# The delta rule's stores and reloads issued from ACT instead of SP, in a hybrid encoder layer

## The chip, the cores and the metric

The kernel runs on one core of a Trainium2 chip. The core has five engines that run their own instruction streams in order: PE (TensorE, matrix products), DVE (VectorE), ACT (ScalarE), POOL (GpSimd) and SP (SyncE, which here issues transfers and computes nothing). Transfers between the chip's large memory (DRAM below) and the engines' memory are carried out by 16 DMA engines; an instruction on SP or ACT only issues them. Engines wait for each other, and for transfers, through semaphores.

The metric is device time in microseconds, from one launch. Before the change three runs gave 1266.28, 1262.38 and 1264.82 us, a median of 1264.82.

## What is computed

One layer over 2048 positions of width 1024, in float32. A normalised input is projected, and the projection is split between two groups of heads that read the same rows. Group A is a gated delta rule with four heads, run forward and backward over the sequence; group B is windowed attention. Both are gated, joined, projected back and added to the input. The change lies in group A, whose core is this:

```python
k_beta = k * beta[..., None]
m = jnp.where(strict, jnp.einsum('bhncd,bhnsd->bhncs', k_beta, k) * decay, 0.0)
t_inv = lax.linalg.triangular_solve(eye + m, eye_like_m, left_side=True, lower=True, unit_diagonal=True)
...
def step(state, inp):
    q_i, k_i, u_i, w_i, g_i, a_i = inp
    v_new = u_i - jnp.einsum('bhcd,bhde->bhce', w_i, state)
    o = (jnp.einsum('bhcd,bhde->bhce', q_i * jnp.exp(g_i)[..., None], state)
         + jnp.einsum('bhcs,bhse->bhce', a_i, v_new))
    ...
_, o = lax.scan(step, state0, xs)
```

For each chunk of the sequence a unit triangular matrix `eye + m` has to be inverted before the scan over chunks can use it. The kernel works with chunks of 128 positions, so 16 chunks, in two directions, for each of four heads.

## The kernel before

**Phase A** (to about 690 us of the profile) projects, convolves and does the attention. It is not touched by the diff, except that its instructions are ordered by the same planner. **Phase B** does the delta rule and the output projection. For each head `h` it has these parts, and the parts of one head are interleaved with the scan of the head before:

- `pre_front(h)`: in four groups of four chunks, transposes k and q, forms Gram products on PE (`gh`), and on DVE the matrices `ma` (L711), which hold for each chunk and direction the decayed `m` and the decayed q-k product. Tiles of `ma` stand also under the names `xhi_h` and `xlo_h` for heads 1 and 3, where they lie in space that phase A has left. L716 stores the `m` part of each group and direction to the DRAM tensor `m_d`: 8 stores a head, 32 in all.
- `solve(h)`: inverts the 32 x 32 diagonal blocks of all chunks at once. Two loads read the blocks back from `m_d`, laid out with one row of blocks to a partition: `X` (L739, forward) and `L` (L740, backward), each in pieces of 32 numbers. Then 31 steps on DVE (L749, L753) solve column by column, and L754 stores the result `X` to the DRAM tensor `x_d`.
- `invert(h)`: for each of four groups, loads the solved blocks of both directions into `xc` (L765, 8 loads a head, 32 in all), spreads them over block-diagonal tiles `iv` (DVE and POOL), and builds the full inverse with products on PE (`pi`, L781) and copies on ACT (`b` L790, `iv` L796 and L802, `ma` L799 and L805).
- `scan(h)`: for 16 chunks in each direction `kqc` is loaded (L819), and then PE, DVE and ACT take turns: `pk`, `r`, `py`, `yk` and `y` (ACT, L835 and L837), `po`, the new state `S`.
- `post(h)`: normalises and gates the scan's output `oacc` and stores it (`zt`, `mix_dn`).

As filler between them stand the late gate projections (`zs`, `zhi`, `pf_z`, up to about 790 us) and units of the attention's output projection: `mxs` (load, L583), `mhs` (ACT) and `mls` (DVE), `pcs` (PE), the residual rows `xrs` (load, L593; added on DVE, L599), `part` (store, L600).

**What sets the order.** The program is recorded in the order of the source. Then `set_order` gives each instruction a modelled cost, and simulates a list of ready instructions per engine, forward and backward in turns. The order that it ends with is fixed for every engine. Before the change all 927 DMAs are on SP. The planner takes 500 for the cost of an instruction of SP, adds a lag until the data are there, and lets one shared bus hold SP back when more than it can move is pending. The built program gives each DMA one of eight semaphores (`DMAHW0` to `DMAHW7`) in rotation, so that a DMA's list of waits may name the semaphore of an earlier transfer beside its own data.

Of the kernel before, what the change touches and what calls it, by code (L numbers as in the profile page):

```python
# [15 lines left out]
P = 128  # L16
# [530 lines left out]
def phase_b(ctx, wide, xe, ae, late, tc, t, ident, consts, hp, mix_dn, mix_sw, kq_d, v_d, zdn_d, zsw_d, dp, out):  # L547
    nc = tc.nc
    V, A, G, T = nc.vector, nc.scalar, nc.gpsimd, nc.tensor
    dma = nc.sync.dma_start  # L550

    def pool(name, bufs=1, stack=ctx, **kw):
        return stack.enter_context(tc.tile_pool(name=name, bufs=bufs, reuse_waits="tile", **kw))
# [87 lines left out]
    def pre_front(h):  # L641
# [9 lines left out]
        ma = H["ma"] = {}  # L651
        m_d = dp.tile([2, NCH, 4 * (32 * P + 32)], F32, tag="m_d", name=f"m_d{h}", bufs=2)
        x_d = dp.tile([2, NCH, P, 32], F32, tag="x_d", name=f"x_d{h}", bufs=2)
        for n, c4 in enumerate(FRONT):
            s4 = slice(4 * c4, 4 * c4 + 4)
            cs = slice(c4 * 512, (c4 + 1) * 512)
            kq = q2[:, 2 * (n % 2) : 2 * (n % 2) + 2]
            dma(kq, kq_d[h][:, :, cs])
            vt = q2[:, 4 + n % 2]
            dma(vt, v_d[h][:, cs])  # L660
            gms = []
            for d in range(2):
                k = 2 * (n % 2) + d
                if k < 3:
                    gm = q3[:, k].rearrange("p (c i) -> p c i", c=4)
                else:
                    gm = q1.tile([P, 4, P], F32, tag="gm", name=f"dc{h}_{c4}_{d}", bufs=1)
                if h < NDEC:
                    dma(gm.rearrange("p c i -> p (c i)"), dec_d[h, d][c4])
                else:  # L670
                    src = gr_d[d].rearrange("(c h) i -> c h i", h=4)[s4, h]
                    dma(gm, src.partition_broadcast(P))
                    G.tensor_tensor(gm, gm, dmask[:, d : d + 1].to_broadcast([P, 4, P]), ALU.add)
                gms.append(gm)
                p = 3 - c4 if d else c4
                if p not in mp:
                    mp[p] = ma_tile(h, p)
                ma[d, c4] = mp[p][:, :, 1 - d :: 2]
            for j, ss in ((0, ssk), (1, ssq)):
                tr = ps_t.tile([P, 4, P], F32, tag="tr", name=f"tr{h}_{c4}_{j}")  # L680
                for c in range(4):
                    T.transpose(tr[:, c], kq[:, j, c * P : (c + 1) * P], ident)
                if j == 0:
                    ks[c4] = kv_tile("ks", h, n, f"ks{h}_{c4}")
                    A.activation(ks[c4], tr, AF.Copy)
                for c in range(4):
                    cc = 4 * c4 + c
                    src = ks[c4] if j == 0 else tr
                    jk = q1.tile([P, P], F32, tag="jk", name=f"jk{h}_{c4}_{j}_{c}", bufs=3)
                    A.activation(jk, src[:, c], AF.Square, accum_out=ss[:, cc : cc + 1])  # L690
            V.tensor_scalar(ssk[:, s4], ssk[:, s4], EPS, None, ALU.add)  # L691
            G.tensor_tensor(nk[:, s4], ssk[:, s4], pw[:, 0, :4], ALU.pow)  # L692
            V.reciprocal(ssk[:, s4], ssk[:, s4])
            V.tensor_tensor(
                bp[:, :, s4], beta[:, s4, h :: 4].rearrange("p c d -> p d c"),
                ssk[:, s4].unsqueeze(1).to_broadcast([P, 2, 4]), ALU.mult,
            )
            for c2 in range(2):
                gh = ps_g.tile([P, 2, 2, P], F32, tag="gh", name=f"gh{h}_{c4}_{c2}")
                for k in range(2):  # L700
                    c = 2 * c2 + k
                    T.matmul(
                        gh[:, k], kq[:, 0, c * P : (c + 1) * P], kq[:, :, c * P : (c + 1) * P], start=True, stop=True
                    )
                for k in range(2):
                    c = 2 * c2 + k
                    cc = 4 * c4 + c
                    for d in range(2):
                        if h >= NDEC:
                            A.activation(gms[d][:, c], gms[d][:, c], AF.Exp, bias=ngc[:, d, cc, h : h + 1])  # L710
                        V.scalar_tensor_tensor(  # L711
                            ma[d, c4][:, c], gh[:, k], bp[:, d, cc : cc + 1],
                            gms[d][:, c : c + 1].to_broadcast([P, 2, P]), ALU.mult, ALU.mult,
                        )
            for d in range(2):
                dma(m_d[d, s4, : P * P].rearrange("u (i j) -> i u j", j=P), ma[d, c4][:, :, 0])  # L716
            tr = ps_t.tile([P, 4, P], F32, tag="tr", name=f"trv{h}_{c4}")
            for c in range(4):
                T.transpose(tr[:, c], vt[:, c * P : (c + 1) * P], ident)
            vs[c4] = kv_tile("vs", h, n, f"vs{h}_{c4}")  # L720
            for c in range(4):
                cc = 4 * c4 + c
                A.activation(vs[c4][:, c], tr[:, c], AF.Copy, scale=nk[:, cc : cc + 1])
            if h:
                for k in range(FILLF[h - 1][n]):
                    fill(1, bank(k % 2))
# [6 lines left out]
    def solve(h, H):  # L733
        m_d, x_d, _ = H["solve"]
        L = qa.tile([P, 32, 32], F32, tag="L", name=f"L{h}")
        X = qa.tile([P, 32, 32], F32, tag="X", name=f"X{h}")
        lv = [m_d[d].rearrange("u (p y) -> (u p) y", p=4)[:, : 32 * P] for d in range(2)]
        lv = [a.rearrange("q (r x) -> q r x", x=P)[:, :, :32] for a in lv]
        dma(X[0:64], lv[0])  # L739
        dma(L[64:128], lv[1])  # L740
        x = X.rearrange("p r c -> p (r c)")
        V.tensor_copy(L[0:64], X[0:64].rearrange("p r c -> p c r"))
        G.memset(x, 0.0)
        G.memset(x[:, ::33], 1.0)
        for c in range(31):
            n = 31 - c
            tm = qa.tile([P, 256], F32, tag="tm", name=f"tm{h}_{c}")
            tv = tm[:, : n * (c + 1)].rearrange("p (r k) -> p r k", k=c + 1)
            V.tensor_tensor(  # L749
                tv, L[:, c + 1 :, c : c + 1].to_broadcast([P, n, c + 1]),  # L750
                X[:, c : c + 1, 0 : c + 1].to_broadcast([P, n, c + 1]), ALU.mult,
            )
            V.tensor_tensor(X[:, c + 1 :, 0 : c + 1], X[:, c + 1 :, 0 : c + 1], tv, ALU.subtract)  # L753
        dma(x_d.rearrange("d u (p r) c -> (d u p) (r c)", p=4), X.rearrange("p r c -> p (r c)"))  # L754

    def invert(h, H):
        _, x_d, mp = H["solve"]
        for hi in range(4):
# [3 lines left out]
            for d, c4 in ((0, hi), (1, 3 - hi)):  # L762
                xc = qb.tile([P, 4, 32], F32, tag="xc", name=f"xc{h}_{d}_{c4}", bufs=4)
                xt = qb.tile([P, 4, 32], F32, tag="xt", name=f"xt{h}_{d}_{c4}", bufs=4)
                dma(xc, x_d[d, 4 * c4 : 4 * c4 + 4].rearrange("u i c -> i u c"))  # L765
                V.transpose(xt.rearrange("p u c -> p (u c)"), xc.rearrange("p u c -> p (u c)"))
                x0[d], x1[d] = (xc, xt) if d == 0 else (xt, xc)
            g = qb.tile([P, 4, P], F32, tag="g", name=f"g{h}_{hi}", bufs=2)
# [276 lines left out]
def set_order(tc):  # L1045
# [12 lines left out]
    def aps(l):  # L1058
        return [a.bass_ap for a in l if hasattr(a, "bass_ap")]
# [138 lines left out]
    def cost(i, eng):  # L1198
        o = aps(i.outs)
        m, ins = size(o[0]), aps(i.ins)  # L1200
        if eng == "SP":
            return 500
        if eng == "PE":
            if i.is_transpose:
# [21 lines left out]
    eng = [e for _, e in insts] + [None] * (total - n)  # L1226
    move, late = [0.0] * total, [0.0] * total
    nxt, prv = [[] for _ in range(total)], [[] for _ in range(total)]
    for k in range(total):
        if eng[k] == "SP":  # L1230
            a = aps(insts[k][0].outs)[0]
            count = a.ap[0][1] * size(a)
            piece = min(run(x) for x in aps(insts[k][0].ins) + [a])
            move[k] = count / piece * (8 + 0.148 * piece) / 16
            spread = [x.ap[0][0] == 0 for x in aps(insts[k][0].ins)]
            late[k] = 2000 * any(spread)
        lag = LAG[eng[k]] + move[k] + late[k] if k < n else 0
        if eng[k] == "PE" and not insts[k][0].is_transpose and "float32r" not in str(insts[k][0].ins[0].dtype):
            lag += 40
        if eng[k] == "Activation" and len(aps(insts[k][0].outs)) > 1:  # L1240
            lag += 90
        for s in succ[k]:
            if eng[s] == eng[k] != "SP":
                nxt[k].append((s, SAME[eng[k]] * ((k, s) in wrote)))
            else:
                nxt[k].append((s, lag))
        for s in started[k] if k < n else ():
            nxt[k].append((s, None))
        for s, d in nxt[k]:
            prv[s].append((k, d))  # L1250
# [30 lines left out]
    def plan(order, forward):  # L1281
# [29 lines left out]
        for _ in range(n):  # L1311
# [13 lines left out]
            if e == "SP":  # L1325
                release(k, max(t, bus))
                bus = max(t, bus) + move[k]
                free[e] = max(free[e], bus - 1000)
            else:
                release(k, t)  # L1330
        end = max(free.values())
# [85 lines left out]
```

## Time and profile before

| | before |
|---|---|
| median of three runs | 1264.82 us (1262.38 to 1266.28) |
| profiled execution, span of the core | 1268.0 us, no other time is shown for it |
| mean granted clock of PE | 0.989 |
| DMAs issued on SP, on ACT | 927, 0 |
| moved by them | 206 MB, 163 GB/s over the span |

The span runs from the first to the last instruction. In the views quoted below, "idle before, releaser" means how long an engine had nothing to do ahead of an instruction, and what ended this. `SPq` is SP's sequencer, whose rows are the issues of DMAs; their length is the time that the issue took, not the time to the data's arrival, which the profile gives as "DMA to landing". Matrix products of the profile overlap, so that a busy PE need not be PE at its best; a granted clock under 1 slows it further. The chain is the work that ended last, followed back from the last instruction: a transfer that stands in it was, at that time, what everything else waited for.

### The profile page before, as it was taken

Reading aid. Unit: us, or ns where it says so; the run is one execution under the profiler, and the core shown is the slowest. Engines: PE = TensorE matmul, PEld = TensorE weight load, DVE = VectorE, ACT = ScalarE, POOL = GpSimd, SP = SyncE. Lnnn points to the kernel's source line nnn. Section 1 sums busy time; section 2 is a strip of 40 time slices with the busy share of each in tenths; the row PEclk is TensorE's granted clock in tenths of the full one; section 3 lists DMA queues with packets and bytes.
Section 4 is the critical chain, followed back from the end, with each engine's and each line's share of the span. In section 5 each row is a group of like instructions: output and inputs, shape, how many; then the busy total and the mean of one; then the engine's idle time right before and its main releaser. Section 6 shows DMA issues by size and latency. Waiting matters only on the chain.

```text
span 1268.0 us, 22351 instructions
## 1 busy us (share of the span) xinstructions
PE 1210.5 (95%) x7018; PEld 1037.4 (82%) x7018; DVE 953.7 (75%) x2320; ACT 725.8 (57%) x2167; POOL 529.2 (42%) x845
## 2 busy tenths in 40 slices
PE   6999999999999999999999998999889899999898
PEld 5998888788889988887777777888789689888776
DVE  4523689999854379999995587698769779876765
ACT  6432476666534367766665438658557845685421
POOL 2243454763302276556422304613742441670541
PEclk9999999999999999999999999999889999999999
DMA  7553243513544434431016848967955875854785
GB/s 259 172 160 125 75 154 100 173 60 102 166 145 125 144 110 137 137 96 55 34 51 207 238 141 245 264 189 207 268 166 174 236 200 152 242 175 122 238 269 199
DMA packets 232294, 206.39 MB, mean 163 GB/s; under 512 B 49137, under 2 KB 181873, under 8 KB 232177
## 3 DMA queue, kind: packets, MB, share of 16 engines
q1 hardware_dynamic: 232176, 204.97, 53.0%
q8 instruction: 56, 0.92, 0.3%
q14 instruction: 62, 0.50, 0.1%
HBM read 139.84 MB, written 65.08 MB: 162 GB/s over the span
## 4 chain that ended last, share of the span: by engine, by line
PE 67%; DVE 13%; DMA 9%; ACT 4%; issue 3%; POOL 1%; SPq 1%; DVEq 0%; ACTq 0%; POOLq 0%
PE pf_c L199 5%; PE pf_c L201 5%; PE pf_c L200 5%; PE pf_z L199 4%; PE pf_z L200 4%; PE pf_z L201 4%; PE pi L781 3%; PE pq_q L212 2%; PE pq_q L211 2%; PE pt L390 2%; PE pq_q L210 2%; DMA xc<-x_d 2%; PE py L830 2%; PE po L839 2%; PE pcs L596 2%
## 5 line engine op out<-in xcount | busy, mean ns | idle before, releaser
L199 PE MATMUL pf_c<-xhi,wh_c 128*128 128x512 f32 x384 | 155.7, 405 | 0.8 <-DVE acc L269 0.8
L200 PE MATMUL pf_c<-xlo,wh_c 128*128 128x512 f32 x384 | 154.7, 403 | 0.0
L201 PE MATMUL pf_c<-xhi,wl_c 128*128 128x512 f32 x384 | 154.3, 402 | 0.0
L269 DVE SCALAR_TENSOR_TENSOR acc<-pf_c,cw,acc 128x512 f32<-128x512 f32 (+1 forms) x192 | 140.8, 742 | 2.6 <-POOL acc L259 0.7
L385 POOL TENSOR_SCALAR pr<-pr,st 128x384 f32<-128x384 f32 (+1 forms) x128 | 79.4, 639 | 98.0 <-DVE st L383 71.2
L394 ACT ACTIVATE ph<-pt 128x512 fp32r<-128x512 f32 x92 | 53.0, 595 | 60.5 <-PE pt L390 51.5
L376 ACT ACTIVATE pr<-pr,st 128x384 f32<-128x384 f32 (+1 forms) x128 | 76.2, 597 | 17.8 <-DVE st L372 17.4
L199 PEld LDWEIGHTS pf_c<-xhi,wh_c 128*128 128x128 f32 x384 | 72.5, 189 | 13.5 <-DVE acc L269 1.3
L201 PEld LDWEIGHTS pf_c<-xhi,wl_c 128*128 128x128 f32 x384 | 72.3, 188 | 12.9
L200 PEld LDWEIGHTS pf_c<-xlo,wh_c 128*128 128x128 f32 x384 | 72.4, 188 | 11.6
L835 ACT ACTIVATE yk<-py,ck 128x128 f32<-128x128 f32 x120 | 43.9, 366 | 62.0 <-PE py L830 61.2
L372 DVE CUSTOM_DVE_ANT_0 pr<-s,mask,sink 128x384 f32<-128x384 f32 (+1 forms) x128 | 73.4, 593 | 2.5 <-PE s L371 1.0
L211 PE MATMUL pq_q<-wh_q,xlo 128*128 128x256 f32 x256 | 72.1, 282 | 0.0
L212 PE MATMUL pq_q<-wl_q,xhi 128*128 128x256 f32 x256 | 71.9, 281 | 0.0
L210 PE MATMUL pq_q<-wh_q,xhi 128*128 128x256 f32 x256 | 71.4, 280 | 0.0
L390 PE MATMUL pt<-ident,pr 128*128 128x128 f32 x368 | 69.5, 274 | 1.8 <-DVE pl L395 1.1
L395 DVE TENSOR_TENSOR pl<-pt,ph 128x512 fp32r<-128x512 f32 x92 | 61.6, 681 | 6.1 <-ACT ph L394 5.6
L390 PEld LDWEIGHTS pt<-ident,pr 128*128 128x128 f32 x368 | 47.8, 140 | 20.4 <-DVE pl L395 4.4
L596 PE MATMUL pcs<-wohs,mhs 128*128 128x512 f32 x128 | 58.3, 456 | 4.4 <-ACT mhs L590 2.7
L692 POOL TENSOR_TENSOR nk<-ssk,pw 128x4 f32<-128x4 f32 x16 | 16.5, 1029 | 106.8 <-DVE ssk L691 106.6
L597 PE MATMUL pcs<-wohs,mls 128*128 128x512 f32 x128 | 56.1, 438 | 1.7 <-DVE mls L591 1.7
L598 PE MATMUL pcs<-wols,mhs 128*128 128x512 f32 x128 | 55.0, 429 | 0.0
(324 smaller groups left out, 4029.4 us busy)
## 6 DMA issues: line engine op xcount, KB each, us to landing
kqc<-kq_d SPq DMA_DIRECT2D x120, 128.0 KB, 3.1
ws_c<-wt SPq DMA_DIRECT2D x48, 256.0 KB, 3.5
xr<-x SPq DMA_DIRECT2D x16, 512.0 KB, 5.3
k_q<-kq_d SPq DMA_DIRECT2D x16, 512.0 KB, 5.6
mxs<-mix_sw SPq DMA_DIRECT2D x32, 256.0 KB, 3.7
xrs<-x SPq DMA_DIRECT2D x32, 256.0 KB, 3.7
part<-xrs SPq DMA_DIRECT2D x32, 256.0 KB, 2.6
xrd<-part SPq DMA_DIRECT2D x32, 256.0 KB, 4.1
```

Source lines behind the costliest of these rows:

```text
L199: T.matmul(ps, hi[:, k, cs], xhi[b][:, k], start=(k == 0), stop=False)
L200: T.matmul(ps, hi[:, k, cs], xlo[b][:, k], start=False, stop=False)
L201: T.matmul(ps, lo[:, k, cs], xhi[b][:, k], start=False, stop=(k == KC - 1))
L210: T.matmul(ps[:, :n], xh, hi[:, k, :n], start=(k == 0), stop=False)
L211: T.matmul(ps[:, :n], xl, hi[:, k, :n], start=False, stop=False)
L212: T.matmul(ps[:, :n], xh, lo[:, k, :n], start=False, stop=(k == KC - 1))
L269: V.scalar_tensor_tensor(av, ps[:, lo:], cw[:, i, k : k + 1], av, ALU.mult, ALU.add)
L372: V.tensor_tensor_reduce(pr[j][:, :n], ps[:, :n], mask[:, lo * P : hi * P], 1.0, sink[:, hh : hh + 1], ALU.add, ALU.min, accum_out=nm[:, j ...
L376: A.activation(pr[j][:, :n], pr[j][:, :n], AF.Exp, bias=nm[:, j : j + 1], scale=-1.0, accum_out=den[:, j : j + 1])
L385: G.tensor_scalar(pr[j][:, :n], pr[j][:, :n], den[:, j : j + 1], 1.0, ALU.mult, ALU.mult)
L390: T.transpose(pt[:, j], pr[j][:, (kb - lo) * P : (kb - lo + 1) * P], ident)
L596: T.matmul(ps, mh[:, k], wh[:, k], start=(k == 0), stop=False)
```

## The change

Five lines of phase B issue their transfers with `nc.scalar.dma_start` in place of `nc.sync.dma_start`: the stores of `m_d`, the loads of `X` and `L`, the store of `x_d` and the loads of `xc`. Sizes, tiles and layouts stay. The planner, which knew a DMA by its engine, now knows it by its kind, and an instruction of this kind on ACT costs 500 there. The bus does not hold ACT back, though its transfers fill it.

```diff
-    dma = nc.sync.dma_start
+    dma, dma2 = nc.sync.dma_start, nc.scalar.dma_start
...
-                dma(m_d[d, s4, : P * P].rearrange("u (i j) -> i u j", j=P), ma[d, c4][:, :, 0])
+                dma2(m_d[d, s4, : P * P].rearrange("u (i j) -> i u j", j=P), ma[d, c4][:, :, 0])
...
-        dma(X[0:64], lv[0])
-        dma(L[64:128], lv[1])
+        dma2(X[0:64], lv[0])
+        dma2(L[64:128], lv[1])
...
-        dma(x_d.rearrange("d u (p r) c -> (d u p) (r c)", p=4), X.rearrange("p r c -> p (r c)"))
+        dma2(x_d.rearrange("d u (p r) c -> (d u p) (r c)", p=4), X.rearrange("p r c -> p (r c)"))
...
-                dma(xc, x_d[d, 4 * c4 : 4 * c4 + 4].rearrange("u i c -> i u c"))
+                dma2(xc, x_d[d, 4 * c4 : 4 * c4 + 4].rearrange("u i c -> i u c"))
...
     def cost(i, eng):
-        if eng == "SP":
+        if "DMA" in str(i.opcode):
             return 500
...
+    moves = [k < n and "DMA" in str(insts[k][0].opcode) for k in range(total)]
...
-        lag = LAG[eng[k]] + move[k] + late[k] if k < n else 0
+        lag = LAG["SP" if moves[k] else eng[k]] + move[k] + late[k] if k < n else 0
...
         for s in succ[k]:
-            if eng[s] == eng[k] != "SP":
+            if eng[s] == eng[k] and not moves[s] and not moves[k]:
                 nxt[k].append((s, SAME[eng[k]] * ((k, s) in wrote)))
...
             if e == "SP":
                 release(k, max(t, bus))
                 bus = max(t, bus) + move[k]
                 free[e] = max(free[e], bus - 1000)
+            elif moves[k]:
+                release(k, t)
+                bus = max(t, bus) + move[k]
             else:
                 release(k, t)
```

The planner orders the whole program anew, so that all five engines' streams differ a little from the start on; the instructions that compute are the same in number. In names like `X1_10276` below, the first number is the head, the last one counts tiles; `[waits ...]` lists semaphores.

First place, the reload of head 1's matrices. On SP before, it stands between the stores of output rows (`part`) and loads for the scan (`kqc`):

```order
L739 DMA X1_10276<-m_d1_9782 64x32x32 [waits DMAHW3_49]
L740 DMA L1_10275<-m_d1_9782 64x32x32 [waits DMAHW4_49]
L600 DMA part0_7713<-xrs0_0_10095 128x512 [waits DMAHW5_49,DVE_49]
L600 DMA part1_7714<-xrs1_0_10118 128x512 [waits DMAHW6_49,DVE_49]
L819 DMA kqc0_1_6_9315<-kq_d0_87 128x2x128 [waits DMAHW7_49,PE_49]
L819 DMA kqc0_0_7_9335<-kq_d0_87 128x2x128 [waits DMAHW0_49,PE_49]
```

On ACT now, at the third step of head 0's scan:

```order
L835 ACTIVATE yk0_0_2_9143<-py0_0_2_9139,ck0_7765 128x128 [waits PE_49,Activation_49]
L573 ACTIVATE wohs0_10071<-woss0_3_10085 128x512 [waits DMAHW0_49]
L837 ACTIVATE y0_0_2_9145<-py0_0_2_9139 128x128 [waits Activation_49]
L739 DMA X1_10276<-m_d1_9782 64x32x32 [waits DMAHW5_49,DMAHW2_49]
L740 DMA L1_10275<-m_d1_9782 64x32x32 [waits DMAHW3_49,DMAHW2_49]
L805 ACTIVATE ma0_1_7771<-pi4_0_1_8908 64x4x64 [waits PE_49]
L835 ACTIVATE yk0_1_2_9163<-py0_1_2_9159,ck0_7765 128x128 [waits PE_49]
L837 ACTIVATE y0_1_2_9165<-py0_1_2_9159 128x128 [waits Activation_49]
```

What stands behind the two loads is no longer transfers, but a copy of head 0's inverse and the scan's `yk` and `y`. `X` and `L` follow each other directly on ACT for heads 0, 2 and 3 as well.

Second place, head 1's solved blocks. On ACT now, the first loads of `xc` come where head 0's scan has ended and head 2's last group is being prepared:

```order
L690 ACTIVATE jk2_3_1_2_11613,ssq2_11357<-tr2_3_1_11604 128x128 [waits Activation_49]
L837 ACTIVATE y0_1_15_9726<-py0_1_15_9722 128x128 [waits PE_49]
L690 ACTIVATE jk2_3_1_3_11615,ssq2_11357<-tr2_3_1_11604 128x128 [waits Activation_49]
L765 DMA xc1_0_0_10376<-x_d1_9783 128x4x32 [waits DMAHW7_49]
L765 DMA xc1_1_3_10380<-x_d1_9783 128x4x32 [waits DMAHW1_49]
L723 ACTIVATE vs2_3_11650<-trv2_3_11645,nk2_11355 128x128 [waits PE_49,Pool_49]
```

On SP before, they stood between the loads of head 3's q, k and v:

```order
L660 DMA k2_q_7735<-v_d3_94 128x512 [waits DMAHW2_49]
L765 DMA xc1_0_0_10376<-x_d1_9783 128x4x32 [waits DMAHW3_49]
L660 DMA k2_q_7735<-v_d3_94 128x512 [waits DMAHW4_49,PE_49]
L765 DMA xc1_1_3_10380<-x_d1_9783 128x4x32 [waits DMAHW5_49]
L658 DMA k2_q_7735<-kq_d3_90 128x2x512 [waits DMAHW6_49,PE_49]
```

The first of the two loads waits for the store of `x_d` to have landed. What stood behind it was prefetch; now it is `vs`, which scales head 2's values.

More of the change, by code (lines that the diff above doesn't have):

```diff
@@ L1228, in set_order @@
     nxt, prv = [[] for _ in range(total)], [[] for _ in range(total)]
+    moves = [k < n and "DMA" in str(insts[k][0].opcode) for k in range(total)]
     for k in range(total):
-        if eng[k] == "SP":
+        if moves[k]:
             a = aps(insts[k][0].outs)[0]
@@ L1236, in set_order @@
             late[k] = 2000 * any(spread)
-        lag = LAG[eng[k]] + move[k] + late[k] if k < n else 0
+        lag = LAG["SP" if moves[k] else eng[k]] + move[k] + late[k] if k < n else 0
         if eng[k] == "PE" and not insts[k][0].is_transpose and "float32r" not in str(insts[k][0].ins[0].dtype):
             lag += 40
-        if eng[k] == "Activation" and len(aps(insts[k][0].outs)) > 1:
+        if eng[k] == "Activation" and not moves[k] and len(aps(insts[k][0].outs)) > 1:
             lag += 90
         for s in succ[k]:
-            if eng[s] == eng[k] != "SP":
+            if eng[s] == eng[k] and not moves[s] and not moves[k]:
                 nxt[k].append((s, SAME[eng[k]] * ((k, s) in wrote)))
```

## The prediction

> **What bounds the kernel now.** I read the page from the top: busy time by engine, then the chain that ended last, then the stages.
>
> ```profile
> PE 1210.5 (95%) x7018; PEld 1037.4 (82%) x7018; DVE 953.7 (75%) x2320; ACT 725.8 (57%) x2167; POOL 529.2 (42%) x845
> PE 67%; DVE 13%; DMA 9%; ACT 4%; issue 3%; POOL 1%; SPq 1%; DVEq 0%; ACTq 0%; POOLq 0%
> ```
>
> PE is the bound: busy for 95% of the span and 67% of the last chain. DMA has 9% of that chain, SP's queue 1%. The change touches only the delta rule's preparation, which runs from about 690 to 1112 us; before and behind it nothing but a new instruction order can move the time. The stage view cuts this part out.
>
> ```profile
> 690.00:770.00 80.00, 77.25 (x361) 62.14 (x360) 54.95 (x155) 38.51 (x152) 14.08 (x13) 1.00 0.67 190
> 770.00:1112.00 342.00, 314.19 (x2088) 279.58 (x2087) 278.81 (x854) 225.98 (x860) 150.35 (x270) 0.97 0.74 214
> 883.00:904.00 21.00, 15.86 (x85) 13.46 (x84) 16.85 (x55) 14.06 (x63) 11.07 (x23) 0.84 0.97 283
> 904.00:990.00 86.00, 80.64 (x558) 73.50 (x557) 69.64 (x208) 56.31 (x215) 37.53 (x58) 0.96 0.67 191
> 990.00:1005.00 15.00, 9.36 (x60) 7.42 (x59) 10.40 (x38) 10.80 (x55) 5.42 (x7) 0.99 0.91 255
> ```
>
> The columns are length, then busy time of PE, weight loads, DVE, ACT, POOL, then granted clock, DMA share, GB/s. Between 770 and 1112 PE is idle 342 - 314.2 = 27.8 us, and the clock, 0.97, takes another 10. Whatever the change can win lies in these 38 us. They bunch: 883 to 904 and 990 to 1005 each lose over 5 us of PE with the DMA engines 97% and 91% busy. ACT is busy 38.5 + 226.0 = 264.5 of 422 us, 63%.
>
> The waits of PE between 770 and 1112 say who ended them:
>
> ```profile
> PE gh L702 <- DVE ma L711: 4.3, 4, 2.6
> PE pi L781 <- DVE iv L776: 3.6, 1, 3.6
> PE pk L821 <- DVE S L842: 3.6, 3, 3.2
> PE pcs L596 <- ACT mhs L590: 2.3, 4, 1.0
> PE trv L719 <- ACT jk L690: 1.9, 3, 0.9
> PE pcs L596 <- ACT xlo_h L723: 1.5, 1, 1.5
> PE po L839 <- ACT yk L835: 1.4, 3, 1.0
> ```
>
> The columns are total, times and longest. The three long ones go to DVE; the four listed for ACT sum to 7.1 us. Behind DVE stand transfers, as the chain shows in order of time (start, length):
>
> ```profile
> 882.43 6.82 DMA x_d<-X
> 889.27 4.05 DMA xc<-x_d
> 924.46 6.88 DMA xrs<-x
> 989.96 6.23 DMA x_d<-X
> 996.21 7.61 DMA xc<-x_d
> ```
>
> At 882 and at 990 the solved blocks go out and come back before the inversion can start. At 924 it is the residual row `xrs`, which the change does not touch, but which stood behind something that it does:
>
> ```profile
> 811.62 4.60 SPq L740 DMA_DIRECT2D L<-m_d  x1
> 914.49 3.90 SPq L740 DMA_DIRECT2D L<-m_d  x1
> 1021.88 3.23 SPq L740 DMA_DIRECT2D L<-m_d  x1
> 726.07 0.60 SPq L740 DMA_DIRECT2D L<-m_d  x1
> ```
>
> The load of `L`, issued right behind the load of `X`, holds the queue for 3.2 to 4.6 us. For head 0, where it went out 4.4 us after `X`, it took 0.6. That speaks for an issue that is held while the transfer ahead of it drains.
>
> **The change, part by part.** 76 DMAs move from SP to ACT: 32 stores of `m_d`, 4 loads each of `X` and `L`, 4 stores of `x_d`, 32 loads of `xc`. No byte is saved. The planner then sets a new order for all five engines; the counts of arithmetic instructions stay.
>
> Issue time on ACT. Nothing in this trace is issued from ACT, so SP's durations are the nearest rows (minimum, median, maximum in ns):
>
> ```profile
> L716 SPq DMA_DIRECT2D m_d<-ma x20: 360/462/922, 691.2 to 1014.1; - x20
> L716 SPq DMA_DIRECT2D m_d<-xhi_h x8: 371/445/682, 767.2 to 1017.5; - x8
> L716 SPq DMA_DIRECT2D m_d<-xlo_h x4: 582/594/782, 787.4 to 1004.6; - x4
> L739 SPq DMA_DIRECT2D X<-m_d x4: 606/606/610, 721.7 to 1021.2; - x4
> L754 SPq DMA_DIRECT2D x_d<-X x4: 325/520/583, 768.1 to 1076.9; - x4
> L765 SPq DMA_DIRECT2D xc<-x_d x32: 359/500/2141, 774.7 to 1105.2; - x32
> ```
>
> 20 x 0.462 + 8 x 0.445 + 4 x 0.594 + 4 x 0.606 + 4 x 0.520 + 32 x 0.500 = 35.7 us, `L` left out. ACT has 157 us of idle time here to take them. Least cost: ACT's share in PE's waits, 7.1 of 226 us busy, 3%, so 1 us. Most: every issue that falls on ACT's busy 63% delays PE in full, 22.5 us. I take 3, near the lower end, since the row of PE's waits on ACT is the nearer one.
>
> The held issue of `L`. In the new order `L` stands directly behind `X` on ACT in all four heads. Behind them stand the inversion's copies and the `yk` and `y` of the scan, for which PE waits at each step. Least: nothing, if ACT would have idled then. Most: the three long holds and as much again for head 0, 4.60 + 3.90 + 3.23 + 4.60 = 16.3 us. For head 1 ACT has idle time at the place:
>
> ```profile
> 812.27 2.22 ACT L710 ACTIVATE v_q<-v_q,ngc 128x128 f32<-128x128 f32 x7 [1.58 <-POOL v_q L673]
> 816.56 0.63 ACT L590 ACTIVATE mhs<-mxs 128x512 fp32r<-128x512 f32 x1 [1.28 <-DMA mxs<-mix_sw]
> ```
>
> It hides 1.58 + 1.28 = 2.9 of the 4.6. I take 2 us for each of heads 1 to 3, 6 in all; at head 0 the late gates run, and their projections keep PE supplied.
>
> New waits on ACT. It now stops for the end of the solve before `x_d`, and for the landing of `x_d` before the first `xc`. For head 1 the new order puts the rows from `vs` to the last `jk` between the two:
>
> ```profile
> 880.73 1.17 ACT L723 ACTIVATE vs<-trv,nk 128x128 f32<-128x128 f32 x4
> 886.35 0.24 ACT L690 ACTIVATION_READ_ACCUMULATOR jk<-tr 128x1 f32 x1
> ```
>
> From 880.73 to 886.35 + 0.24 they fill 5.9 us, and `x_d` took 6.8 to land: 1 us of waiting, with `vs` queued behind. Least: 0, if `x_d` lands faster. Most, for heads 1 to 3: all that the landing can exceed the cover, up to 6.8 each, 20 us. I take 1 us each, 3 in all, by head 1's rows.
>
> Half-clock spells. The stages with long PE gaps are also those with a granted clock under 1 (0.84 x 21 us and 0.96 x 86 us each cost 3.4 us). I add 3 us for new gaps; least 0, most 2 x 3.4.
>
> Losses: 3 + 6 + 3 + 3 = 15 us, between 1 and 22.5 + 16.3 + 20 + 6.8 = 66 if nothing of it overlapped.
>
> What goes, first: the landings. How long the blocks took (`x_d` store, then `xc` loads; minimum, median, maximum):
>
> ```profile
> DMA to landing us min/median/max: 3.1/6.4/6.8
> DMA to landing us min/median/max: 2.2/4.0/7.6
> ```
>
> The fastest `x_d`, 3.1, is head 3's, in a stage with less traffic. [...] PE's gaps at these places, and at the `xrs` one, with idle time and releaser in brackets:
>
> ```profile
> 896.11 2.05 PE L781 MATMUL pi<-iv,g 128*128 128x128 f32 x8 [3.64 <-DVE iv L776]
> 1001.16 0.50 PE L596 MATMUL pcs<-wohs,mhs 128*128 128x512 f32 x1 [1.52 <-ACT xlo_h L723]
> 1004.69 1.56 PE L702 MATMUL gh<-k_q 128*128 128x256 f32 x3 [2.57 <-DVE ma L711]
> 934.11 0.80 PE L821 MATMUL pk<-S,kqc 128*128 128x128 f32 x2 [3.24 <-DVE S L842]
> ```
>
> If heads 1 and 2 landed at the fastest rows, both gaps would close: 3.64 + 1.52 + 2.57 = 7.7 us, and 3.4 of clock: 11. If the DMA engines, 97% busy, are the limit, nothing. I take the middle, 6. Late next at head 1 would be ACT's copy `b`:
>
> ```profile
> 898.85 1.43 PE L781 MATMUL pi<-b,iv 128*128 128x128 f32 x5 [0.69 <-ACT b L790]
> ```
>
> [...]
>
> What goes, second: SP's holds. Without 3.90 us at 914 `xrs` goes out earlier and the gap of 3.24 with its 3.4 us of clock may close: at most 6.6. The holds of heads 1 and 3 have no PE gap of that size behind them. I take 4; least 0, since the same bytes still pass the same engines.
>
> Sum: 15 - 6 - 4 = +5 us. The trace gives the execution's span alone, 1268.0 us, 3.2 above the median of the three runs and 1.7 above the highest; no own time beside it is shown. 1268.0 + 5 = 1273 there, so 1264.8 + 5 = **1270 us** against the median.
>
> **The rivals.**
>
> A, faster, with its own mechanism: the second queue lets the blocks overtake. `x_d` plus `xc` took 6.82 + 4.05 = 10.9 us at head 1 and 6.23 + 7.61 = 13.8 at head 2; the fastest rows give 3.1 + 2.2 = 5.3. It decides for a gain from the point where both fall under about 7: then the gaps close (11 us) and the 6.6 behind `xrs` too, against ACT's losses with their waits gone, 3 + 3. 11 + 6.6 - 6 = 11.6, so 1264.8 - 11.6 = 1253. For it: head 3's 3.1, and ACT's 37% of idle time. Against: the DMA engines are over 90% busy just where it would count.
>
> [...]
>
> B, no difference: PE has other work (the output projection's `pcs`) at nearly every place, losses and gains are both covered, and the time stays at 1265. For it: PE waits for ACT and DVE at these places for a few us only.
>
> C, clearly slower: in the new order most DMAs on ACT also wait for a DMA semaphore that a transfer of SP signals, beside their own data (45 such waits, counted in the built program), and 54 of SP's wait for one of ACT's. An engine that computes then waits for loads that are none of its business, and the scan's `kqc` wait for ACT. If 30 of the 45 cost PE half a microsecond each, 15 us, on top of the forecast's 5: 1285. It decides once ACT's waits for DMA pass some 20 us. Against: each of them stands some eight DMAs back in the built order, so that most should have landed by then.
>
> That the change does not do what it says can be put aside: the 76 DMAs stand on ACT in the built order.
>
> **How the numbers follow.** The forecast, a small loss with 1265 to 1276 as its own range, 0.36. A 0.30, B 0.16, C 0.18. 0.3% is 3.8 us, about what a measurement of this kernel can tell from no change: within it, 1261.0 to 1268.6, lie B and some 0.10 of the forecast. So faster 0.30, the same 0.26, slower 0.44. A falls at 1253 with a spread of some 6, C at 1285 with as much; leaving 1 in 10 out on each side gives 1250 to 1290. The bound of 66 is not reached by it, since ACT's holds and waits overlap and have 157 us of idle time to fall into.
>
> **What would show it.** ACT's sequencer rows should show about 0.5 us for each moved DMA and 3 to 5 for `L`; an `L` of 0.6 us would strike the 6 us. PE's waits for ACT's `yk`, `ma` and `b` should grow from a few us to about 10. `x_d` to landing under 4 us with the gap at the inversion gone would speak for A; ACT waits for DMAs of SP as long rows in its own list for C. SP's rows should show no hold of 3 us at `xrs` or `part`. The prediction is wrong in kind if PE's idle time between 690 and 1112 falls, and beside the point if the difference lies before 690 us, where only the order has changed.

## The result, and the profile after

The changed kernel is slower: 1281.54 us (median of four runs, 1278.74 to 1282.16) against 1263.60 us for the kernel before, run beside it (four runs, 1261.79 to 1266.28). The ratio is 1.0145, with a 95% interval of 1.011 to 1.018, so +18 us. (Below, a difference in us is the ratio less 1, times 1263.) The profiled executions differ by less, 1279.7 against 1268.0 us of span: the earlier one lies 4.4 us above its median, the later one 1.8 below. The earlier kernel's span of 1268.0 us is above every span of its executions that were timed beside the experiments (1253.2 to 1266.0 us), so that losses read against its trace come out some 6 to 10 us too small below, and a gap that stands in it need not stand in most executions.

From the page of the changed kernel, busy time by engine, the transfer queue that is new (packets, MB, share of 16 engines' time) and the chain that ended last:

```profile
PE 1214.4 (95%) x7018; PEld 1036.7 (81%) x7018; DVE 958.6 (75%) x2320; ACT 725.9 (57%) x2167; POOL 529.1 (41%) x845
q10 hardware_dynamic: 50880, 14.68, 4.7%
PE 64%; DVE 12%; DMA 10%; ACT 7%; issue 3%; POOL 2%; SPq 1%; ACTq 0%; DVEq 0%; POOLq 0%
```

The counts of arithmetic are the same as before, and so is ACT's busy time, 725.9 for 725.8 us. `q10` is the new queue, with the 14.68 MB of the moved transfers and 4.7% of the 16 engines' time; SP's `q1` has 47.4%, after 53.0% before. ACT's part of the last chain grew from 4 to 7%, but ACT's sequencer, where the 76 issues now stand, has 0%.

Where is the time lost? First the span of the kernel before in three pieces, then that of the changed one (columns as in the prediction):

```profile
0.00:690.00 690.00, 674.42 (x3763) 575.01 (x3764) 515.59 (x1091) 390.78 (x934) 302.74 (x486) 1.00 0.39 125
690.00:1112.00 422.00, 391.44 (x2448) 341.72 (x2447) 333.76 (x1008) 264.49 (x1011) 164.44 (x283) 0.97 0.73 210
1112.00:1300.00 188.00, 144.59 (x811) 120.64 (x810) 104.37 (x223) 70.50 (x225) 61.98 (x77) 0.99 0.53 167
```

```profile
0.00:690.00 690.00, 672.00 (x3745) 572.08 (x3746) 513.46 (x1082) 387.60 (x909) 302.43 (x485) 1.00 0.39 125
690.00:1112.00 422.00, 385.27 (x2398) 333.58 (x2397) 333.11 (x996) 260.35 (x1004) 158.32 (x269) 0.97 0.71 207
1112.00:1300.00 188.00, 157.12 (x876) 131.04 (x876) 112.00 (x243) 77.92 (x256) 68.35 (x92) 0.98 0.55 177
```

PE does 2.4 us less up to 690 and 6.2 us less in the stage that the change touches (36.7 us idle there instead of 30.6), and is busy 3.9 us longer in all; behind 1112 it idles 0.8 us less. That makes the 11.7 us between these two executions: over half of it is PE's idle time between 690 and 1112, and a fifth lies ahead of 690. The granted clock in the stage is 0.97 in both. The changed kernel comes to the same work later: it stores `x_d` of head 1 at 892.1 us in place of 882.4, and of head 2 at 1009.1 in place of 990.0. So the rows that answer to the prediction's 883 to 904 and 990 to 1005 are cut from these stores on; the first row and the last one are cut at the same times in both:

```profile
690.00:770.00 80.00, 74.17 (x344) 58.30 (x344) 49.88 (x137) 38.11 (x153) 14.24 (x13) 1.00 0.63 179
...
892.70:913.70 21.00, 17.91 (x111) 14.98 (x110) 18.82 (x65) 15.13 (x68) 10.01 (x17) 1.00 1.00 287
...
1009.10:1024.10 15.00, 11.79 (x46) 8.92 (x45) 11.04 (x36) 7.72 (x36) 6.50 (x11) 0.81 0.64 184
...
1005.00:1035.00 30.00, 25.30 (x123) 19.87 (x122) 17.70 (x54) 16.85 (x67) 15.81 (x35) 0.84 0.79 213
```

Of the two places that the prediction expected to gain, head 1's inversion did: PE is busy 17.91 us in place of 15.86, at a clock of 1.00 for 0.84, and its gap of 3.64 us at the inversion is one of 0.54:

```profile
906.55 1.13 PE L781 MATMUL pi<-iv,g 128*128 128x128 f32 x8 [0.54 <-DVE iv L776]
```

At head 2 PE is busy 11.79 us in place of 9.36, but the clock there is 0.81 for 0.99, which takes about as much again. And 3.1 us are gone ahead of 770 (74.17 for 77.25). Between 1005 and 1035 the changed kernel is at head 2's reload, which the kernel before has behind it by then; its row there:

```profile
1005.00:1035.00 30.00, 28.14 (x167) 24.09 (x166) 22.32 (x61) 17.17 (x58) 18.25 (x46) 0.95 0.80 215
```

The issues on ACT, in ns (minimum, median, maximum), and under the rows of `x_d` and of `xc` the time to landing in us:

```profile
L716 ACTq DMA_DIRECT2D m_d<-ma x20: 366/412/732, 702.0 to 1019.8; - x20
...
L739 ACTq DMA_DIRECT2D X<-m_d x4: 616/627/659, 737.3 to 1027.4; - x4
L740 ACTq DMA_DIRECT2D L<-m_d x4: 1207/1814/2017, 738.0 to 1028.1; - x4
L754 ACTq DMA_DIRECT2D x_d<-X x4: 338/338/339, 782.4 to 1082.5; - x4
DMA to landing us min/median/max: 2.6/3.6/4.3
L765 ACTq DMA_DIRECT2D xc<-x_d x32: 366/408/2032, 785.0 to 1114.5; - x32
DMA to landing us min/median/max: 1.9/4.5/7.8
```

Each issue takes about 0.4 us of ACT's sequencer, `L` about 1.8. But ACT's arithmetic goes on meanwhile, as its timeline shows (start, length; ACTq is the sequencer):

```profile
785.00 0.36 ACT L723 ACTIVATE vs<-trv,nk 128x128 f32<-128x128 f32 x1
785.03 0.37 ACTq L765 DMA_DIRECT2D xc<-x_d  x1
785.25 0.36 ACT L723 ACTIVATE vs<-trv,nk 128x128 f32<-128x128 f32 x1
785.44 0.53 ACTq L765 DMA_DIRECT2D xc<-x_d  x1
785.50 0.62 ACT L723 ACTIVATE vs<-trv,nk 128x128 f32<-128x128 f32 x2
786.00 0.41 ACT L710 ACTIVATE v_q<-v_q,ngc 128x128 f32<-128x128 f32 x1
786.01 0.64 ACTq L716 DMA_DIRECT2D m_d<-xhi_h  x1
```

Three issues, 1.5 us together, leave no hole between `vs` and `v_q`. PE's waits between 770 and 1112, those for ACT of 0.9 us and over among them:

```profile
PE pi L781 <- DVE iv L776: 3.0, 2, 2.5
PE po L839 <- DVE zt L890: 2.7, 1, 2.7
PE tr L682 <- DMA k_q<-kq_d: 2.5, 2, 2.2
PE pcs L596 <- DVE xhi_h L711: 2.2, 1, 2.2
...
PE pi L781 <- ACT b L790: 1.5, 3, 0.7
PE po L839 <- ACT yk L835: 1.5, 2, 0.8
...
PE tr L682 <- ACT ks L685: 1.0, 2, 0.8
...
PE pcs L596 <- ACT mhs L590: 0.9, 2, 0.5
```

These four for ACT sum to 4.9 us. Summed over the whole list, PE's waits for ACT went from 8.7 to 7.4 us, those for DVE from 17.5 to 19.6 and those for transfers from 0.3 to 2.5; what grew are waits for things that come late in the new order: loads of k and q (`k_q`), the end of a head's scan (`zt`), the matrices (`xhi_h`).

### The profile page after: what moved, and what is told of

It is laid out like the page before. It is cut to its first block, busy times and chain, and to the rows that moved or that the text cites. A ratio compares the mean times of both kernels' runs of the same rounds, so it can differ in the third digit from the quotient of the medians.

```text
span 1279.7 us, 22399 instructions
## 1 busy us (share of the span) xinstructions
PE 1214.4 (95%) x7018; PEld 1036.7 (81%) x7018; DVE 958.6 (75%) x2320; ACT 725.9 (57%) x2167; POOL 529.1 (41%) x845
## 3 DMA queue, kind: packets, MB, share of 16 engines
q1 hardware_dynamic: 181296, 190.29, 47.4%
q10 hardware_dynamic: 50880, 14.68, 4.7%
## 4 chain that ended last, share of the span: by engine, by line
PE 64%; DVE 12%; DMA 10%; ACT 7%; issue 3%; POOL 2%; SPq 1%; ACTq 0%; DVEq 0%; POOLq 0%
PE pf_c L200 4%; PE pf_c L199 4%; PE pf_c L201 4%; PE pi L781 4%; PE pf_z L201 3%; PE pf_z L199 3%; PE pf_z L200 3%; DMA xc<-x_d 3%; PE pt L390 3%; DVE acc L269 2%; PE pq_q L212 2%; PE pq_q L211 2%; PE pq_q L210 2%; PE py L830 2%; PE pcs L596 2%
## 5 line engine op out<-in xcount | busy, mean ns | idle before, releaser
L201 PEld LDWEIGHTS pf_c<-xhi,wl_c 128*128 128x128 f32 x384 | 72.3, 188 | 12.7
L200 PEld LDWEIGHTS pf_c<-xlo,wh_c 128*128 128x128 f32 x384 | 72.5, 189 | 11.7
```

Of the source, the lines that this page charges most:

```text
L200: T.matmul(ps, hi[:, k, cs], xlo[b][:, k], start=False, stop=False)
L201: T.matmul(ps, lo[:, k, cs], xhi[b][:, k], start=False, stop=(k == KC - 1))
```

## The experiments

Two theories stand against each other: the time is lost by **the new order**, which the planner makes for all five engines, or by **the issue on ACT**, through ACT's time, the held `L`, and waits of DMAs in ACT's row. Each run was timed in five rounds against the kernel before.

In the table, "planned" is the engine on which the planner puts the moved DMAs, "issued" that which really issues them. "PE's gaps" sums all gaps of PE over 0.3 us in the profiled execution. "Late" is worked out from the trace: each PE instruction is weighted with the median time that its like takes in the trace of before, and the column says how many us later than there the same share of this work was done, at 790 and at 1030 us of the earlier trace (good to about 0.5 us).

| kernel | planned, issued | ratio, 95% interval | us | PE's gaps | late at 790, 1030 |
|---|---|---|---|---|---|
| before | SP, SP | | | 38.9 | |
| changed | ACT, ACT | 1.0145 [1.0110, 1.0180] | +18 | 48.0 | 13.1, 13.7 |
| order_alone | ACT, SP | 1.0161 [1.0137, 1.0185] | +20 | 55.5 | 14.1, 15.1 |
| issue_alone | SP, ACT | 1.0103 [1.0080, 1.0127] | +13 | 42.3 | 7.8, 7.0 |
| blocks_act | `x_d`, `xc` on ACT, both | 1.0148 [1.0123, 1.0174] | +19 | 48.1 | 6.6, 14.9 |
| jitter_520 | SP, SP; 520 ns | 1.0051 [1.0032, 1.0070] | +6 | 41.2 | 6.3, 1.9 |
| jitter_480 | SP, SP; 480 ns | 1.0046 [1.0028, 1.0064] | +6 | 43.3 | 9.0, 5.9 |
| new_then_old | new order to head 0's scan, SP | 1.0069 [1.0046, 1.0093] | +9 | 41.0 | 12.7, 6.1 |
| old_then_new | new order from head 0's scan, SP | 1.0037 [1.0019, 1.0056] | +5 | 43.1 | -0.1, -2.9 |
| blocks_issue | SP; `x_d`, `xc` issued on ACT | 1.0052 [1.0033, 1.0071] | +7 | 38.2 | 3.4, -0.7 |
| mats_issue | SP; `m_d`, `X`, `L` issued on ACT | 1.0056 [1.0038, 1.0075] | +7 | 41.8 | 3.1, 3.2 |
| after_480 | ACT, ACT; 480 ns | 1.0170 [1.0147, 1.0193] | +21 | 46.9 | 4.5, 19.8 |
| act_bus | ACT, ACT; bus counted | 1.0097 [1.0070, 1.0124] | +12 | 40.7 | 15.9, 5.1 |
| bus_480 | ACT, ACT; both | 1.0172 [1.0140, 1.0205] | +22 | 50.6 | 10.7, 13.7 |

### The order without the issue, and the issue without the order

order_alone keeps the changed kernel's order and gives all DMAs back to SP; what was planned for ACT and now goes to SP is merged into SP's row by its planned start (one of the five lines is shown):

```diff
-                dma2(m_d[d, s4, : P * P].rearrange("u (i j) -> i u j", j=P), ma[d, c4][:, :, 0])
+                dma(m_d[d, s4, : P * P].rearrange("u (i j) -> i u j", j=P), ma[d, c4][:, :, 0])
...
+    real = [e for _, e in insts]
+    insts = [(i, planned(i, e)) for i, e in insts]
...
-        for a, b in zip(queue[e], queue[e][1:]):
+        mine = list(heapq.merge(*([k for k in q if real[k] == e] for q in queue.values()), key=lambda k: begin[k]))
+        for a, b in zip(mine, mine[1:]):
```

> The changed kernel's order on PE, DVE and POOL and of ACT's arithmetic, row for row, but all 76 DMAs issued from SP, merged into its queue by the times that the plan gave them. Theory I (the issue from ACT costs the time: ACT is held, and ACT and SP wait for each other's transfers): about the time of before, 1260 to 1268 us. Theory O (the new order is what is slower): about that of the change, 1277 to 1286. A value between them shares the 18 us out.

Measured: +20 us. The order alone is enough for the whole loss; with it given, the issue on ACT adds nothing that can be told apart (1.0145 against 1.0161, with overlapping intervals).

issue_alone is the converse: `planned` returns SP for every DMA, so that each engine's row is the earlier kernel's, and the 76 DMAs go out on ACT at the places where the plan started them on SP.

> The order of before on PE, DVE and POOL and of ACT's arithmetic, row for row, with the 76 DMAs issued from ACT, merged into its order by the times that the plan gave them on SP. Theory I: 1277 to 1286 us. Theory O: 1258 to 1268. If the landings of the solved blocks at heads 1 and 2 shorten as they did at head 1 in the changed kernel, and nothing else happens, some 5 us under before.

Measured: +13 us, between the two theories' ranges. So the issue on ACT is not free as such, and the two causes don't add: 20 and 13 apart, 18 together. Its timeline shows part of the price directly. ACT first, at head 0's scan:

```profile
820.62 4.03 ACTq L740 DMA_DIRECT2D L<-m_d  x1
820.84 0.68 ACT L710 ACTIVATE v_q<-v_q,ngc 128x128 f32<-128x128 f32 x2
824.70 1.28 ACT L710 ACTIVATE v_q<-v_q,ngc 128x128 f32<-128x128 f32 x4 [3.18 <-issue]
825.88 0.35 ACT L855 ACTIVATE oacc<-po,egc 128x128 f32<-128x128 f32 x1
```

Then PE:

```profile
826.61 0.49 PE L832 MATMUL po<-S,kqc 128*128 128x128 f32 x2 [3.49 <-DVE oacc L856]
```

The issue of `L` is held for 4.03 us. ACT finishes the 0.68 us of `v_q` that it already had, and then stands still for 3.18 us until the issue ends at 824.65; `oacc`, queued behind, comes late to DVE, and PE loses 3.49 us. A store of `m_d` that waits until 897.62 to go out does the like at the end of that scan: `jk`, and `y` behind it, stand still until then. Again ACT and then PE:

```profile
897.62 0.36 ACTq L716 DMA_DIRECT2D m_d<-ma  x1
898.03 0.31 ACT L690 ACTIVATE jk<-ks 128x128 f32<-128x128 f32 x1 [1.93 <-DMA m_d<-ma]
...
898.70 0.27 ACT L837 ACTIVATE y<-py 128x128 f32<-128x128 f32 x1
```

```profile
899.02 0.49 PE L848 MATMUL po<-y,ma 128*128 128x128 f32 x2 [2.27 <-ACT y L837]
```

The two gaps sum to 5.8 us, of a difference of 13. The rest is not traced to single issues; by the table 7.8 us are already lost at 790 us, before either gap.

### The issue by halves

blocks_issue and mats_issue are issue_alone with half of the moves:

```diff
-                dma2(m_d[d, s4, : P * P].rearrange("u (i j) -> i u j", j=P), ma[d, c4][:, :, 0])
+                dma(m_d[d, s4, : P * P].rearrange("u (i j) -> i u j", j=P), ma[d, c4][:, :, 0])
...
-        dma2(X[0:64], lv[0])
-        dma2(L[64:128], lv[1])
+        dma(X[0:64], lv[0])
+        dma(L[64:128], lv[1])
```

for the first; for the second, `x_d` and `xc` in the same way.

> The earlier kernel's order row for row, but x_d's four stores and the 32 loads of xc go out on ACT, while m_d, X and L stay on SP. If the 13 us of all 76 DMAs on ACT in this order come of the matrices' stores and of L held on ACT's sequencer (an m_d store that waits keeps y of a scan behind it, and L0's issue of 4 us stands ahead of ACT's copies): 0 to +4 us. If they come of the loads of the blocks, whose waits for a free xc buffer stand in ACT's row: +9 to +13 us. If x_d and xc land sooner on ACT's queue and PE's gap at 930 us goes, it may end 2 to 5 us below the kernel before.

> The earlier kernel's order row for row, but only m_d's 32 stores and X's and L's loads go out on ACT, while x_d and xc stay on SP. If the matrices' DMAs are what costs in this order: +9 to +13 us; if the blocks' are: 0 to +4 us. If neither half alone costs more than 4 us, the loss of 13 us needs both (SP and ACT wait for each other's DMAs, or the clock falls to half where both fall together).

Measured: +7 and +7, which together make the 13. Both expectations missed: they gave 9 or more to one half and 4 at most to the other, and neither half is the culprit alone. blocks_issue also answers a question of the prediction, whether `x_d` lands sooner when ACT issues it, in an order that is otherwise the same:

```profile
L754 ACTq DMA_DIRECT2D x_d<-X x4: 338/340/364, 768.6 to 1072.6; - x4
DMA to landing us min/median/max: 3.6/6.5/7.5
```

A median of 6.5 us on ACT (6.6 in issue_alone) stands against 6.4 on SP, each of four stores. In order_alone, with the new order and SP, it was shorter:

```profile
DMA to landing us min/median/max: 3.2/4.1/4.9
```

So the faster landing of the changed kernel, 3.6 us, comes with the new order's place for the store, mostly, and not with the queue.

### Only the blocks moved, and planned so

blocks_act undoes the moves of `m_d`, `X` and `L` in the kernel and in the plan (the first diff of the halves, without another edit).

> Only the stores of x_d and the loads of xc on ACT, planned so; m_d, X and L stay on SP. If the loss sits in the stores of m_d and the loads of X and L, which in the changed kernel came 10 to 16 us later for head 0: 1256 to 1266 us. If xc on ACT is what costs (xc stood in the chain of head 0 three times): 1272 to 1284.

Measured: +19 us, as with all of them, and in the second range. The loss does not need the matrices' transfers on ACT. How much of it is order and how much issue, this run does not tell.

### Is it any new order?

The planner's result moves with small numbers. In jitter_520 and jitter_480 all DMAs stay on SP, and the order is computed anew with

```diff
-            return 500
+            return 520
```

or 480, which moves thousands of rows.

> The kernel before with one number of the planner moved: 520 in place of 500 for an instruction of SP. All DMAs on SP; only the order differs, by about as many rows as with the change. Theory I: within 4 us of before. Theory O in its form of chance (any new order of this program lands some 10 us to either side): off by more than 5 us.

> The kernel before with one number of its planner changed: a DMA on SP is planned at 480 ns in place of 500, so that the order is computed anew with all DMAs on SP. If the earlier order is a lucky draw among many of like quality: +3 to +20 us, as 520 gave +5. If the new order's 20 us come of what the planner is told of ACT (500 ns per DMA, no bus that holds it back): -3 to +6 us, as the planner here is told the same but for 4%.

Measured: +6 and +6; the second fits both of its ranges and decides nothing between them. Against these two draws the earlier order is a good one, and a new order may by itself cost some 6 us here. That is a third of the 18; two draws don't say how far others would lie. The converse, the changed kernel at 480:

> The changed kernel (76 DMAs on ACT) with every DMA planned at 480 ns in place of 500: another draw of the new kind of order. If its loss is systematic: +14 to +22 us on the kernel before, as the changed kernel. If the loss is the draw: anywhere between +3 and +25 us, and 5 us or more away from the changed kernel's +18.

Measured: +21. Another order for the moved DMAs, and about the same loss, with the issue on ACT in it as in the changed kernel.

### Where in the order

Two hybrids, all DMAs on SP: one plan up to the first product `py` of head 0's scan, the other behind it.

```diff
+    cut = min(first[k] for k, (i, _) in enumerate(insts) if i.outs and hasattr(i.outs[0], "bass_ap") and i.outs[0].bass_ap.tensor.name.startswith("py0_"))
+    key = [(0, first[k]) if first[k] < cut else (1, then[k]) for k in range(len(insts))]
+        mine = sorted((k for k in range(len(insts)) if real[k] == e), key=lambda k: key[k])
```

> All DMAs issued from SP as before; each engine runs the changed kernel's order up to the start of head 0's scan and the earlier kernel's order behind it. Theory 1 (the new order loses in head 0's preparation, which it puts some 10 us later, so that head 0's inversion runs when the late gates' filler is used up): +13 to +18 us on the kernel before, with PE's work already 12 to 15 us late at 790 us and no more lost after that. Rival (any order computed anew costs some us at many places, the stages behind as much as this one): +6 to +10 us.

> The converse, all DMAs from SP: the earlier kernel's order up to the start of head 0's scan and the changed kernel's order behind it. Theory 1: +3 to +7 us, PE's work no more than 3 us late at 790 us and what is lost lost between 1000 and 1035 us (head 2's preparation). Rival: +10 us or more, spread over the stages of heads 1 to 3.

Measured: +9, in the rival's range, and +5, in Theory 1's. Theory 1 there was right that new_then_old is 12 to 15 us late at 790 (12.7), and wrong that this stays: the earlier order behind it brings half of it back (6.1 at 1030). old_then_new is not late at 1030 at all. So neither half holds the loss, and being late at 790 does not decide: act_bus is 15.9 late there and 5.1 at 1030. The last column shows a cleaner mark. The five runs at +18 to +22 are 13.7 to 19.8 us late at 1030 and have 46.9 to 55.5 us of PE gaps; all others are 7.0 late at most, with 38.2 to 43.3. At that place, the preparation of the last head, three of the late runs stand before a load for 2 us or more at once (2.2 in the changed kernel, 5.6 in after_480). order_alone:

```profile
1010.35 1.12 PE L682 MATMUL tr<-ident,k_q 128*128 128x128 f32 x4 [5.33 <-DMA k_q<-kq_d]
```

PE's waits for this load between 690 and 1130 (total, times, longest) were, in the kernel before, the changed one, order_alone and act_bus, in this order:

```profile
PE tr L682 <- DMA k_q<-kq_d: 1.3, 2, 1.1
```

```profile
PE tr L682 <- DMA k_q<-kq_d: 4.6, 4, 2.2
```

```profile
PE tr L682 <- DMA k_q<-kq_d: 7.4, 3, 5.3
```

```profile
PE tr L682 <- DMA k_q<-kq_d: 0.4, 1, 0.4
```

It is one part of the loss and not in every one of the five: after_480 waits 8.0 us for it, but bus_480 only 1.2 and blocks_act 2.1.

### What the planner is told

The changed planner lets a DMA on ACT land without regard to what the bus still carries. act_bus counts it:

```diff
             elif moves[k]:
-                release(k, t)
+                release(k, max(t, bus))
                 bus = max(t, bus) + move[k]
```

> The changed kernel, whose planner lets a DMA on ACT land without regard to what the bus still carries; here such a DMA waits for the bus in the plan as one on SP does, and only ACT itself isn't held back. If the missing bus makes the new order bad (the planner takes the blocks for early and fills the head's preparation too late): +4 to +12 us on the kernel before. If the 500 ns on ACT are what shifts the order: +14 to +22 us, with x_d of head 0 stored at 780 to 784 us again. If the loss is the draw, between +3 and +25 us with no relation to either.

Measured: +12, at the edge of the first range and 6 us below the changed kernel. One draw of an order proves little, so the pair was repeated at 480 ns:

> The changed kernel with both edits of the two runs before it: 480 ns per DMA, and a DMA on ACT that waits for the bus in the plan. It differs from the 480 ns run by the bus alone. If the bus that the planner no longer counts is what costs: +4 to +13 us on the kernel before, 6 us or more below the 480 ns run without it, as with 500 ns. If the first pair's 7 to 9 us were the chance of two draws: +14 us or more, or less than 4 us below the 480 ns run.

Measured: +22, no better than its partner's +21. So the 6 us of the first pair can't be put down to the bus: they may be the chance of two orders, and that the missing bus is the cause is not shown.

No run beat the kernel before.

## Why the prediction was right, and where it was not

The forecast was +5 us, slower, in a range of 1250 to 1290 us. The sign and the range held; the size was off by 13 us, and the term that was missing is the largest one. That the sign held was luck: in the changed kernel the losses on ACT that the sum counts came to little, as the terms below show, some of its gains came, and what made the kernel slower, 20 us in order_alone without any issue on ACT, is not in the sum. The range held because rival C had stretched it upwards, by a mechanism that did not come either.

**The step that failed** is the sentence "The planner then sets a new order for all five engines; the counts of arithmetic instructions stay", which put the new order at no cost, and kept a difference by order alone for the time ahead of 690 us and behind 1112. By order_alone the order is worth 20 us; in the changed kernel PE's windows show 2.4 of its loss ahead of 690 and the rest behind. Two orders planned with all DMAs on SP gave +6 each; five different ones planned with DMAs on ACT gave +18, +19, +21, +12 and +22, a mean of 18. By their ratios the two groups lie apart, though the lowest of the second has an interval that reaches the first. What separates them, about 12 us, is not settled. For the changed order it is the order itself, since order_alone has the loss without an issue on ACT. For the other four, order and issue were not taken apart, and the 6 us of a new draw with the 13 of issue_alone would make as much. Why the changed order is worse than the two draws on SP stays open too: it may be one of the planner's inputs (500 ns of ACT's time for an issue, where at 785 us three of 0.37 to 0.64 us left no hole in ACT's arithmetic; the missing bus; the waits in ACT's row), or the chance of one draw.

**Issue time on ACT, 3 us.** An issue took 0.34 to 0.63 us in place of the 0.44 to 0.61 taken: 20 x 0.412 + 4 x 0.627 + 4 x 0.338 + 32 x 0.408 = 25 us for the rows shown, without `L` and the stores from `xhi_h` and `xlo_h`. In the changed kernel PE's waits for ACT's `yk`, `b` and the like did not grow to 10 us, so nothing of it shows on the path. In the earlier order it is otherwise: this term and the next two sum to 12 us, and issue_alone measured 13, with whatever the second queue gained in it; but of the 13 only 5.8 were traced to holds and waits, so that the near agreement proves no single term.

**The held `L`, 6 us.** It was held 1.2 to 2.0 us in the changed kernel, less than forecast. At head 1 a hold of 2.02 us stopped ACT for 1.86, but no wait of PE for ACT stands behind it at heads 1 to 3, for which the term was taken; it is about nothing there. That a hold can cost PE time is shown once: in issue_alone one of 4.03 us was followed by a gap of PE of 3.49.

**New waits on ACT, 3 us.** Here ACT has waits for DMA as before, and the largest is an old one. ACT, between 690 and 1130 us, before and then after:

```profile
ACT zhi L240 <- DMA zs<-wt: 25.3, 18, 4.5
```

```profile
ACT zhi L240 <- DMA zs<-wt: 20.8, 11, 6.2
```

Rival C, whose 1285 us came nearest to the result, wanted new waits of some 20 us for DMAs that are none of ACT's business; they did not come: the rows of ACT's waits for DMA that are new sum to 6.0 us. The time agrees with C, the mechanism does not. One old wait did take a new victim, since `X` and `L` of head 0 now stand behind it:

```profile
737.21 0.42 ACT L240 ACTIVATE zhi<-zs 128x256 fp32r<-128x256 f32 x1 [4.45 <-DMA zs<-wt]
737.27 0.66 ACTq L739 DMA_DIRECT2D X<-m_d  x1
738.03 1.73 ACTq L740 DMA_DIRECT2D L<-m_d  x1
```

But order_alone, with `X` on SP, loads it at 736.2 too, so that this costs about 1 us; and PE waited 0.95 us for a `zhi` that came behind the held `L`.

**Half-clock spells, 3 us.** The clock between 690 and 1112 stayed at 0.97; the spells moved from head 1's reload and inversion (0.84 to 1.00) to head 2's (0.99 to 0.81). The granted clock was 0.50 at 896 to 902 before and at 1006 to 1014 in the changed kernel; the products `pi` from `iv` and `g` took a mean of 437 ns in the first of these, for 275 at 905 to 930. The term was nothing in sum there.

**The landings, 6 us gained, and SP's holds, 4.** Counted from the stores on, PE gained 17.91 - 15.86 = 2.1 us of busy time at head 1 and 11.79 - 9.36 = 2.4 at head 2; the clock gave 21 x 0.16 = 3.4 at head 1 and took 15 x 0.18 = 2.7 at head 2. That is some 5 us against the 6 of the term. But no run shows the term itself, a landing that is sooner because ACT issues the transfer: in the unchanged order `x_d` landed in 6.5 us when ACT issued it (blocks_issue) beside 6.4 on SP, and with the new order in 4.1 on SP (order_alone). So it was the order. For the same reason rival A, in which the second queue lets the blocks overtake, found no support. The 4 us for SP's hold rested on the gap of 3.24 us at 934, and no run shows that the hold made it: in blocks_issue, with the earlier order and `L` still held for 3.47 us on SP, that gap is gone. What differs there is that DVE waits 0.68 us ahead of its `xrs`, in place of 4.23; the landing of 6.88 us was the longest of that load in the trace of before.

**Rival B** took it that PE has other work at nearly every place. For the issue in the new order that held; for the order it did not, since the order is what says where the other work stands.

## What to carry to other kernels

Where a planner or scheduler sets the order, a change of engine is two changes, and the second, the new order, must be priced by itself: run the new order with the old issue, and the old order with the new issue, and compute the order anew with a number that means nothing, to know how much a mere new draw costs (6 us here in each of two draws). Three short issues on ACT, of 0.37 to 0.64 us, left no hole in its arithmetic here; what could be traced were a hold of 4.03 us and a wait until 897.62, with PE's gaps of 3.49 and 2.27 us behind them, each in front of something short of slack, a copy or a `y` for which the scan's chain was waiting. Compare the same work and not the same times, once one kernel runs late. One variant that comes out better than another is not a cause found while each variant also draws a new order: repeat the pair with another draw.

## What was not expected of the hardware

In these traces ACT's sequencer ran ahead of its arithmetic. Issues of 0.37 to 0.64 us left no hole (785.03 to 786.65, above), while a hold of 4.03 us stopped ACT for 3.18 us once the 0.68 us of work that had been handed over was done, and one of 2.02 us in the changed kernel for 1.86. So in these places the short issues were hidden by the work already queued, and the long ones only by that much: 0.85 of 4.03 us, 0.16 of 2.02.

How long the issue of `L` was held on SP went with its distance from `X` in two runs. In the kernel before it took 0.60 us where it went out 4.4 us after `X`, and 3.2 to 4.6 directly behind it. In order_alone, on the same engine, one other issue happens to stand between the two for heads 1 to 3, and for all four `L` goes out 2.5 to 4.0 us after `X`; no `L` was held:

```profile
L740 SPq DMA_DIRECT2D L<-m_d x4: 601/607/858, 740.1 to 1033.0; - x4
```

In blocks_issue, with the order of before, the issue on SP took 0.59 to 4.80 us again. That fits the prediction's reading, an issue held while the transfer ahead of it drains, which no view shows directly. On ACT it is less plain: directly behind `X` it took 1.2 to 2.0 us in the changed kernel but up to 5.4 in after_480, in issue_alone 4.03 at 2.2 us behind `X` and 0.58 at 3.5. A run with this distance as its only edit was not made.
